# Seven-product steps, PSUM banks and token sums in a two-layer hybrid attention trunk

## The chip, the cores and the metric

The kernel runs on one core of one Trainium2 chip, as one launch. The metric is the device time of that core in microseconds (us), lower is better. A core has TensorE (PE), VectorE (DVE), ScalarE (ACT), GpSimd (POOL) and SyncE (SP), which issues most of the transfers, each with its own queue of instructions. PE writes its results into eight PSUM banks of 128 x 512 float32.

## The reference, cut to what matters

Two layers over 256 tokens of width 2048. In each layer one combined input projection feeds two groups of eight heads; their outputs are joined by an output projection; a SwiGLU block with inner width 5632 follows.

```python
for l in range(DEPTH):                       # 2
    h = rms_norm(x, pre_mix_norm[l])
    proj = h @ w_in[l]                       # 2048 -> 6144: q_sb, k_sb, v_sb, q_d, k_d, v_d
    o_sb = rms_norm(stick_breaking(q_sb, k_sb, v_sb), sb_out_norm[l])
    o_d = rms_norm(differential(rope(q_d), rope(k_d), v_d), diff_subln[l]) * (1 - lam_init)
    x = x + rms_norm(concat(o_sb, o_d) @ w_o[l], post_mix_norm[l])
    h = rms_norm(x, pre_ffn_norm[l])
    x = x + rms_norm((silu(h @ w_gate[l]) * (h @ w_up[l])) @ w_down[l], post_ffn_norm[l])
```

Stick-breaking attention needs, per pair of heads, scores, a log of the kept share, a product with a triangle of ones and an exponential. Differential attention needs two softmax maps per head, their difference, and a transpose of it before the product with v.

## The kernel before

**Products.** All projections are done in float32 by three products each. A weight block of 128 x 1024 (one K pair, that is two K tiles, of a chunk of 512 output columns) is loaded by one transfer of 512 KB into one of four `raw` buffers. ACT rounds it to `hi` (L247), DVE makes `lo` = raw - hi (L249), and `product` (L900) multiplies hi by hi, lo by hi and hi by lo (L903 to L905).

**Eight or seven.** Two chunks are worked together as a pair: for one K pair there are 2 token tiles x 2 chunks x 2 K tiles = 8 block products, 24 instructions (`eight_in`, L757). A Strassen-like form does it in seven, 21 instructions (`seven_in`, `seven_products`, L884 and L920). The seven need sums of weights (`mixed_weights`, L212: five operations of 512 columns and two of 1024 on DVE besides the lo of the first block, L225 to L232, L249, and the roundings on ACT, L221), sums of tokens made once per layer and K pair (`pair_forms` and `token_sums`, L767 and L907; in gate and up `pair_sums`, L1003), and four more banks `extra` for parts that several outputs share. `shared_part` (L937) brings these out once per pair (L940 to L944), and `settle` adds them to the accumulators (L794).

**Input projection.** `mixer_in` (L774) goes through six chunk pairs (`PAIRS`), each with eight K pairs. `IN_NOW[l][n]` lists the K pairs done as seven: none, three, two, two, two, none in layer 0; in layer 1 the first pair has two as well. Within pairs after the first, `IN_ORDER` puts 4, 5, 6 third to fifth. `opening` (L684) does the first pair of layer 0 and makes the token sums of that layer.

**Attention in between.** Attention runs as generators beside the projection. `tick` (L418) is called four times per K pair (every six or so products) and moves on each generator whose time has come: `flip` (L810) transposes q or k of a chunk, `stick_weights` (L536) and `diff_weights` (L594) make the weights of a head pair or a head, `attend` (L514) multiplies them by v, `norm_pair` (L478) normalizes and transposes the result into `mix`. A number that is yielded is a pause in ticks (2 without one). `run_until` in the output projection calls `tick` until the heads of the next K pair are in `mix`.

**PSUM.** Four banks are accumulators (`acc`), three are for passing use (`b`), one (`o`) is for attention's outputs. The sevens of the input projection take all three `b` and the `o`. `clear(n)` (L411) tells a generator whether n ticks are left before the next sevens start (`burst`). `claims[0]` lets one set of weights hold its two score banks at a time, `claims[1]` one attention output. Flips and other transposes take a bank without asking whether one is free.

**Gate and up.** Eleven chunk pairs; the first one works in the order `FIRST_ORDER` with kp 4 and 6 as seven, the first two K pairs being done ahead. `FORM_AT` says at which place among the remaining six (3, 2, 7, 4, 6, 5) the token sums of which K pair are issued.

**Order.** The program's text gives each instruction a place, but on each engine instructions whose inputs are expected to be ready are drawn forward past waiting ones; a stretch of the output projection has ACT and DVE kept in written order (L977), and `high_priority` moves the ends of chunks forward. `weights` (L257) feeds four blocks ahead.

Of the kernel before, what the change touches and what calls it, by code (L numbers as in the profile page):

```python
# [32 lines left out]
TAIL = 3  # L33
KP_O = (4, 5, 6, 7, 0, 1, 2, 3)
PAIRS = ((6, 8), (10, 7), (9, 0), (11, 2), (1, 3), (4, 5))
IN_SEVEN = (4, 5, 6)
IN_ORDER = (0, 1, 4, 5, 6, 2, 3, 7)
IN_NOW = tuple((first, (4, 5, 6), (4, 5), (4, 5), (4, 5), ()) for first in ((), (5, 6)))
SEVEN = (2, 4, 5, 6)
FIRST_SEVEN = (4, 6)  # L40
FIRST_ORDER = (0, 1, 3, 2, 7, 4, 6, 5)
FORM_AT = {1: 4, 2: 6, 4: 5, 5: 2}
DOWN_SEVEN = (3, 6, 9, 12, 15, 18)

WARM = 13
# [9 lines left out]
def weight_order():  # L55

    order = []

    def queue_pair(name, l, kp, c):
        order.append((name, l, kp, c))  # L60
        return len(order) - 1

    plan = []
    sevens, plain = set(), set()
    for l in range(L):
        lay = {"in": {}, "o": {}, "gate": {}, "up": {}, "down": {}}
        for n, (ca, cb) in enumerate(PAIRS):
            for kp in IN_ORDER if n else range(KT // 2):
                lay["in"][ca, kp] = queue_pair("w_in", l, kp, ca)
                lay["in"][cb, kp] = queue_pair("w_in", l, kp, cb)  # L70
                if kp in IN_NOW[l][n]:
                    plain.add(lay["in"][cb, kp])
        order_o = [(c, kp) for kp in KP_O for c in (0, 1)]
        order_o += [(c, kp) for c in (2, 3) for kp in range(KT // 2)]
        lay["order_o"] = order_o
        for c, kp in order_o:
            lay["o"][c, kp] = queue_pair("w_o", l, kp, c)
        for c in range(FF // CW):
            for kp in FIRST_ORDER if c == 0 else range(KT // 2):
                lay["gate"][c, kp] = queue_pair("w_gate", l, kp, c)  # L80
                lay["up"][c, kp] = queue_pair("w_up", l, kp, c)
                if kp in (FIRST_SEVEN if c == 0 else SEVEN):
                    sevens.add(lay["up"][c, kp])
        for half in range(2):
            for kp in range(FF // P // 2):
                for c in (2 * half, 2 * half + 1):
                    lay["down"][c, kp] = queue_pair("w_down", l, kp, c)
                if kp in DOWN_SEVEN:
                    sevens.add(lay["down"][2 * half + 1, kp])
        plan.append(lay)  # L90
    return order, plan, sevens, plain
# [48 lines left out]
def kernel(  # L140
# [264 lines left out]

    clock = [0]
    running = []
    burst = [None]
    claims = [0, 0]

    def clear(n):  # L411

        return burst[0] is None or clock[0] + n <= burst[0]

    def start(gen, n=1):
        running.append([clock[0] + n, gen])
# [61 lines left out]
    def norm_pair(pool, ob, mix, mixed, h0, gcol, nm):  # L478
        ss = small.tile([P, 4], F32, tag="oss", name=f"oss_{nm}")
        for i in range(4):  # L480
            junk = pool.tile([P, CW], F32, tag="t2", name=f"jo_{nm}_{i}")
            nc.scalar.activation(junk[:, 0:P], ob[:, i * P : (i + 1) * P], AF.Square, accum_out=ss[:, i : i + 1])
        yield
        rs = small.tile([P, 4], F32, tag="ors", name=f"ors_{nm}")
        rsqrt(rs, ss, 1.0 / P, nm)
        on = pool.tile([P, 4, P], F32, tag="t2", name=f"on_{nm}")
        nc.vector.tensor_tensor(
            out=on, in0=ob.rearrange("p (i d) -> p i d", i=4), in1=rs.unsqueeze(2).to_broadcast([P, 4, P]), op=ALU.mult
        )
        claims[1] -= 1  # L490
        yield
        yield
        while not clear(2):
            yield 1
        for j in range(2):
            mix[h0 + j] = pool.tile([P, 2, S], F32R, tag="mix" + nm[0], bufs=NH, name=f"mix_{nm}_{j}")
        pb = bank(f"oT_ps_{nm}")
        for i in range(4):
            nc.tensor.transpose(pb[:, i * P : (i + 1) * P], on[:, i, :], ident)
        for j in range(2):  # L500
            nc.scalar.activation(
                mix[h0 + j][:, 0, :], pb[:, j * S : (j + 1) * S], AF.Copy, scale=gains[:, gcol + j : gcol + j + 1]
            )
            nc.vector.scalar_tensor_tensor(
                out=mix[h0 + j][:, 1, :],
                in0=pb[:, j * S : (j + 1) * S],
                scalar=gains[:, gcol + j : gcol + j + 1],
                in1=mix[h0 + j][:, 0, :].bitcast(F32),
                op0=ALU.mult,
                op1=ALU.subtract,  # L510
            )
            mixed.add(h0 + j)

    def attend(pool, kind, l, g, st, mix, mixed):  # L514

        for hp in range(2):
            while (hp, 1) not in st["w"] or "v" not in st or claims[1] or not clear(4):
                yield 1
            claims[1] += 1
            nm = f"{kind}{l}_{g}_{hp}"  # L520
            ob = ps.tile([P, CW], F32, tag="o", bufs=1, name=f"o_{nm}")
            v = st["v"]
            for j in range(2):
                cols = slice((2 * hp + j) * P, (2 * hp + j + 1) * P)
                w = st["w"][hp, j]
                o0 = ob[:, j * S : j * S + P]
                o1 = ob[:, j * S + P : (j + 1) * S]
                nc.tensor.matmul(o0, w[0], v[:, 0, cols], start=True, stop=True)
                nc.tensor.matmul(o1, w[1], v[:, 0, cols], start=True, stop=False)
                nc.tensor.matmul(o1, w[2], v[:, 1, cols], start=False, stop=True)  # L530
            yield
            h0 = g * 4 + 2 * hp
            g0 = (64 if kind == "sb" else 80) + l * NH + h0
            yield from norm_pair(pool, ob, mix, mixed, h0 + (0 if kind == "sb" else NH), g0, nm)

    def stick_weights(pool, l, g, st):  # L536
        q, k = st["q"], st["k"]
        for hp in range(2):
            nm = f"sb{l}_{g}_{hp}"
            while claims[0] or not clear(10):  # L540
                yield 1
            claims[0] += 1
            za, zb = bank(f"za_{nm}"), bank(f"zb_{nm}")
            za3 = za.rearrange("p (h q) -> p h q", h=2)
            zb3 = zb[:, 0:S].rearrange("p (h q) -> p h q", h=2)
# [36 lines left out]
            nc.scalar.activation(w[:, 0 : 2 * S], za, AF.Exp)  # L582
            nc.scalar.activation(w[:, 2 * S : 2 * S + S], zb[:, 0:S], AF.Exp)
            yield
            claims[0] -= 1
            yield
            for j in range(2):
                st["w"][hp, j] = (
# [5 lines left out]
    def diff_weights(pool, l, g, st, j):  # L594

        q, k = st["q"], st["k"]
        for hp in range(2):
            h = 2 * hp + j
            nm = f"df{l}_{g}_{h}"
            while claims[0] or not clear(4):  # L600
                yield 1
            claims[0] += 1
            sc = [bank(f"s{m}_{nm}") for m in range(2)]
            for qt in range(2):
                for m in range(2):
# [31 lines left out]
                        accum_out=sm[:, c : c + 1],  # L637
                    )
            yield
            claims[0] -= 1  # L640
            nc.vector.reciprocal(sm, sm)
            nc.vector.tensor_tensor(out=sm, in0=sm, in1=lamsign[:, l, :], op=ALU.mult)
            for qt in range(2):
# [9 lines left out]
                )  # L653
            yield
            yield
            while not clear(2):
                yield 1
            tp = bank(f"pT_{nm}")
            for b in range(3):
# [114 lines left out]
    def mixer_in(pool, l, rs, xT, mix, mixed):  # L774
# [6 lines left out]

        for n, cc in enumerate(PAIRS):
            banks = [acc_bank(f"in{l}_{c}_{t}") for t in range(NT) for c in cc]
            mine = IN_NOW[l][n]
            w, toks = None, {}

            def settle(t):
# [22 lines left out]
            def flip(c, toks):  # L810
# [5 lines left out]
                key = "q" if kind in (0, 3) else "k"  # L816
                tT = st[key] = pool.tile([P, 4, S], F32, tag="qk", bufs=4, name=f"{key}T{l}_{c}")
                for t in range(NT):
                    while not clear(2):
                        yield 1  # L820
                    pb = bank(f"qkT_ps{l}_{c}_{t}")
                    for j in range(4):
                        nc.tensor.transpose(pb[:, j * P : (j + 1) * P], toks[c, t][:, j * P : (j + 1) * P], ident)
                    nc.scalar.copy(tT[:, :, t * P : (t + 1) * P], pb.rearrange("p (h q) -> p h q", h=4))
                    yield 1
                st[key + "done"] = True
                if "qdone" in st and "kdone" in st:
                    if kind < 3:
# [9 lines left out]
            else:  # L838
# [3 lines left out]
                for j, kp in enumerate(kps):  # L842
# [2 lines left out]
                        sums_of(IN_SEVEN[j - 2])  # L845
                    if kp in mine:
                        if extra is None:
                            assert claims[0] == 0
                            extra = four_banks(True, [f"{q}_in{l}_{n}" for q in ("p1", "p6", "p7", "q5")])
                        seven_in(banks, extra, forms[kp], xT, l, cc, kp, kp == mine[0], kp == mine[-1])  # L850
                        if kp == mine[-1]:
                            burst[0] = None
                            w = pool.tile([P, 4, CW], F32, tag="gpost", bufs=1, name=f"w{l}_{n}")
                            shared_part(extra, [w[:, i, :] for i in range(4)])
                            if n + 1 < len(PAIRS) and IN_NOW[l][n + 1]:
                                burst[0] = clock[0] + 4 * (len(kps) - 1 - j) + 4 * IN_ORDER.index(IN_NOW[l][n + 1][0])
                            else:
                                pool.end_of_sums()
                        continue
# [18 lines left out]
            wait = 3  # L878
            for c in cc:
                if c // 2 not in (2, 5):  # L880
                    start(flip(c, toks), wait if c // 2 < 3 else wait + 6)
                    wait += 2

    def seven_in(banks, extra, sums, xT, l, cc, kp, first, last):  # L884
        hi, lo = weights(plan[l]["in"][cc[0], kp], LOOKAHEAD)
# [339 lines left out]
```

## Time and profile before

| what | value |
|---|---|
| device time, median of 3 runs | 2235.07 us (2230.51 to 2238.75) |
| device time of the profiled execution | 2233.99 us |
| its span, first to last instruction | 2232.3 us |
| granted TensorE clock, mean | 0.996 |
| input projection of layer 0 / layer 1 | 6.8 to 309.4 us / 1110.4 to 1422.5 us |
| gate and up start, layer 0 / layer 1 | 404.3 us / 1517.4 us |
| HBM read, written | 456.47 MB, 8.39 MB |

A row of a group of instructions names the line, engine and operation, the tile written and the tiles read, shape, count, busy time and mean duration in ns, and the idle time of the engine before them with what ended it. A row of waits reads "engine and instruction <- what it waited for: us in total, times, longest". A row of windows gives the busy time and the count of instructions of each engine in that stretch. The chain of waits ends with PE at 77% of the span, DVE at 13% and transfers at 4%. Idle time of an engine that does not set the end costs nothing.

### The profile page before, as it was taken

To read this page: it belongs to the slowest core of one execution; us is meant where nothing else is said; L and a number is where in the kernel's file an instruction comes from. 1 tells how busy PE (TensorE), PEld (TensorE's weight loads), DVE (VectorE), ACT (ScalarE), POOL (GpSimd) and SP (SyncE) were. 2 spreads that over 40 slices of the span, in tenths; PEclk is the share of its full clock that TensorE was granted. 3 is DMA by queue.
4 is the path that set the end of the run, shared out by engine and by line. 5 is a ranking of instruction groups with operands and counts; after the bars stand their busy time and mean duration, and the time that the engine had idled before them with its cause. 6 is when DMAs were issued, how large, how long until landed. Compare 5 with 4: busy or idle time off the path is not lost.

```text
span 2232.3 us, 28660 instructions
## 1 busy us (share of the span) xinstructions
PE 2192.2 (98%) x9997; PEld 1790.3 (80%) x9997; DVE 1896.3 (85%) x2718; ACT 1363.4 (61%) x2041; POOL 137.6 (6%) x184
## 2 busy tenths in 40 slices
PE   9999999999999999999989999999999999999998
PEld 7777888778888888888867778887788888888886
DVE  7888655899999998989899886558999999989897
ACT  7666654656655656656666666546566566566663
POOL 1100000000000000000002000000000000000000
PEclk9999999999999999999999999999999999999999
DMA  8555655787776675767455556557867767757673
GB/s 288 171 170 164 214 189 183 227 256 220 224 248 212 221 245 188 243 205 240 156 183 162 172 173 200 184 191 237 248 212 233 234 213 232 234 193 246 198 254 100
DMA packets 138081, 466.75 MB, mean 209 GB/s; under 512 B 15824, under 2 KB 16336, under 8 KB 137424
## 3 DMA queue, kind: packets, MB, share of 16 engines
q1 hardware_dynamic: 120512, 430.30, 56.4%
q0 software_dynamic: 15552, 28.32, 7.7%
q10 hardware_dynamic: 1872, 6.31, 0.7%
q8 instruction: 78, 1.28, 0.2%
q14 instruction: 67, 0.55, 0.1%
HBM read 456.47 MB, written 8.39 MB: 208 GB/s over the span
## 4 chain that ended last, share of the span: by engine, by line
PE 77%; DVE 13%; DMA 4%; issue 3%; ACT 2%; SPq 0%; DVEq 0%; ACTq 0%
PE c L904 8%; PE c L905 8%; PE c L903 8%; PE in L903 5%; PE in L905 5%; PE in L904 5%; PE dn L1109 4%; PE dn L1110 4%; PE dn L1112 4%; DMA raw<-in_weights_in_turn_dram 4%; DVE lo L249 4%; PE o L441 3%; PE o L443 3%; PE o L442 3%; PE p L903 2%
## 5 line engine op out<-in xcount | busy, mean ns | idle before, releaser
L249 DVE TENSOR_TENSOR lo<-raw,hi 128x1024 fp32r<-128x1024 f32 x546 | 657.7, 1223 | 164.8 <-ACT hi L247 163.9
L247 ACT ACTIVATE hi<-raw 128x1024 fp32r<-128x1024 f32 x546 | 565.5, 1053 | 254.0 <-DMA raw<-in_weights_in_turn_dram 75.5
L903 PE MATMUL c<-hi,xF 128*128 128x512 f32 x820 | 323.0, 396 | 4.3 <-DVE w L944 2.2
L904 PE MATMUL c<-lo,xF 128*128 128x512 f32 x820 | 320.4, 392 | 3.7 <-DVE lo L249 3.7
L905 PE MATMUL c<-hi,xF 128*128 128x512 f32 x820 | 319.7, 392 | 0.0
L207 POOL DMA_DIRECT2D T<-in_weights_in_turn_dram x108 | 94.1, 871 | 1671.4 <-DMA T<-in_weights_in_turn_dram 560.4
L903 PEld LDWEIGHTS c<-hi,xF 128*128 128x128 f32 x820 | 154.1, 188 | 37.7 <-ACT hi L247 3.3
L904 PEld LDWEIGHTS c<-lo,xF 128*128 128x128 f32 x820 | 155.0, 189 | 35.2 <-DVE lo L249 4.6
L905 PEld LDWEIGHTS c<-hi,xF 128*128 128x128 f32 x820 | 154.9, 189 | 32.7
L1109 PE MATMUL dn<-hi,jh 128*128 128x512 f32 x464 | 180.7, 389 | 0.0
L1110 PE MATMUL dn<-lo,jh 128*128 128x512 f32 x464 | 180.5, 389 | 0.0
L249 DVE TENSOR_TENSOR lo<-G,hi 128x1024 fp32r<-128x1024 f32 x108 | 131.7, 1220 | 27.8 <-ACT hi L247 27.7
L221 ACT ACTIVATE Th<-T 128x512 fp32r<-128x512 f32 x108 | 67.6, 626 | 128.0 <-DVE T L228 128.0
L1112 PE MATMUL dn<-hi,jl 128*128 128x512 f32 x464 | 142.9, 389 | 0.0
L222 DVE TENSOR_TENSOR lo<-T,hi 128x1024 fp32r<-128x1024 f32 x108 | 131.7, 1220 | 12.1 <-ACT hi L221 11.5
L222 DVE TENSOR_TENSOR Tl<-G,Th 128x1024 fp32r<-128x1024 f32 x108 | 131.7, 1220 | 9.3 <-ACT Th L221 9.2
L221 ACT ACTIVATE hi<-T 128x1024 fp32r<-128x1024 f32 x108 | 113.3, 1049 | 42.3 <-PE c L905 25.1
L221 ACT ACTIVATE Th<-G 128x1024 fp32r<-128x1024 f32 x108 | 113.9, 1054 | 39.1 <-DVE G L230 38.9
L903 PE MATMUL in<-hi,xT 128*128 128x512 f32 x321 | 128.2, 401 | 0.3 <-ACT xT L695 0.3
L903 PE MATMUL in<-hi,xI 128*128 128x512 f32 x307 | 123.3, 405 | 4.4 <-DVE w L794 3.4
L904 PE MATMUL in<-lo,xT 128*128 128x512 f32 x321 | 125.9, 392 | 0.7 <-DVE lo L249 0.7
L905 PE MATMUL in<-hi,xT 128*128 128x512 f32 x321 | 125.7, 392 | 0.0
(376 smaller groups left out, 4705.6 us busy)
## 6 DMA issues: line engine op xcount, KB each, us to landing
raw<-in_weights_in_turn_dram SPq DMA_DIRECT2D x566, 512.0 KB, 4.5
T<-in_weights_in_turn_dram SPq DMA_DIRECT2D x108, 512.0 KB, 4.5
G<-in_weights_in_turn_dram SPq DMA_DIRECT2D x108, 512.0 KB, 4.7
T<-in_weights_in_turn_dram POOLq DMA_DIRECT2D x108, 256.0 KB, 6.4
away_ffn<-x ACTq DMA_DIRECT2D x8, 512.0 KB, 5.4
xd<-away_ffn SPq DMA_DIRECT2D x8, 512.0 KB, 9.3
xr<-in_x_columns_dram SPq DMA_DIRECT2D x8, 256.0 KB, 6.4
x<-in_x_dram SPq DMA_DIRECT2D x8, 256.0 KB, 6.5
```

The source lines that it names most:

```text
L207: nc.gpsimd.dma_start(sums[i][:, 0, :], stream[i - 1][:, 0, :], accum_op=ALU.add)
L221: nc.scalar.activation(h, w, AF.Copy)
L222: nc.vector.tensor_tensor(out=l, in0=w, in1=h.bitcast(F32), op=ALU.subtract)
L247: nc.scalar.activation(hi, raw, AF.Copy)
L249: nc.vector.tensor_tensor(out=lo, in0=raw, in1=hi.bitcast(F32), op=ALU.subtract)
L441: nc.tensor.matmul(a, sh, hi[:, kk, :], start=first and kk == 0, stop=False)
L903: nc.tensor.matmul(a, sh, hi, start=first, stop=False)
L904: nc.tensor.matmul(a, sh, lo, start=False, stop=False)
L905: nc.tensor.matmul(a, sl, hi, start=False, stop=last)
L1109: nc.tensor.matmul(accs[c, t], sh, hi[:, kk, :], start=first, stop=False)
L1110: nc.tensor.matmul(accs[c, t], sh, lo[:, kk, :], start=False, stop=False)
L1112: nc.tensor.matmul(accs[c, t], sl, hi[:, kk, :], start=False, stop=last)
```

## The change

K pair 6 is no longer done as seven in the second chunk pair of both layers, and K pairs 5 and 6 no longer in the first chunk pair of layer 1, so that `IN_NOW` is the same in both layers: two K pairs in each of the four middle chunk pairs. Token sums of the input projection are made for K pairs 4 and 5 alone.

`claims` goes. `taken` lists until which tick each `b` bank is counted as held, and `banks_for(n, ticks, held)` lets a generator go on only if n more fit into three and `clear(ticks)` holds. A bank for a transpose counts for two ticks; the two of a set of weights count until `give_back`, and one tick more. Flips ask for each of their two banks and pause two ticks after each, and start later: the second of a pair three ticks after the first instead of two, and for the differential heads 4 x (number of sevens in the next pair) ticks later. After the last seven of a pair, `clear` is false for `SETTLE` = 2 ticks.

In the first chunk pair of gate and up the token sums of K pairs 4 and 6 are issued one place later; those of 5 and 2 stay.

```diff
 TAIL = 3
 KP_O = (4, 5, 6, 7, 0, 1, 2, 3)
 PAIRS = ((6, 8), (10, 7), (9, 0), (11, 2), (1, 3), (4, 5))
-IN_SEVEN = (4, 5, 6)
+IN_SEVEN = (4, 5)
 IN_ORDER = (0, 1, 4, 5, 6, 2, 3, 7)
-IN_NOW = tuple((first, (4, 5, 6), (4, 5), (4, 5), (4, 5), ()) for first in ((), (5, 6)))
+IN_NOW = ((), IN_SEVEN, IN_SEVEN, IN_SEVEN, IN_SEVEN, ())
+SETTLE = 2
 SEVEN = (2, 4, 5, 6)
 FIRST_SEVEN = (4, 6)
 FIRST_ORDER = (0, 1, 3, 2, 7, 4, 6, 5)
-FORM_AT = {1: 4, 2: 6, 4: 5, 5: 2}
+FORM_AT = {2: 4, 3: 6, 4: 5, 5: 2}
 DOWN_SEVEN = (3, 6, 9, 12, 15, 18)
 
 WARM = 13
...
             for kp in IN_ORDER if n else range(KT // 2):
                 lay["in"][ca, kp] = queue_pair("w_in", l, kp, ca)
                 lay["in"][cb, kp] = queue_pair("w_in", l, kp, cb)
-                if kp in IN_NOW[l][n]:
+                if kp in IN_NOW[n]:
                     plain.add(lay["in"][cb, kp])
         order_o = [(c, kp) for kp in KP_O for c in (0, 1)]
         order_o += [(c, kp) for c in (2, 3) for kp in range(KT // 2)]
...
 
     clock = [0]
     running = []
-    burst = [None]
-    claims = [0, 0]
+    burst = [None, 0]
+    attending = [0]
 
     def clear(n):
 
-        return burst[0] is None or clock[0] + n <= burst[0]
+        return clock[0] >= burst[1] and (burst[0] is None or clock[0] + n <= burst[0])
+
+    taken = []
+
+    def banks_for(n, ticks, held=False):
+
+        taken[:] = [until for until in taken if until > clock[0]]
+        if len(taken) + n > 3 or not clear(ticks):
+            return False
+        taken.extend([math.inf if held else clock[0] + 2] * n)
+        return True
+
+    def give_back():
+        taken[:] = [clock[0] + 1 if until == math.inf else until for until in taken]
 
     def start(gen, n=1):
         running.append([clock[0] + n, gen])
...
         nc.vector.tensor_tensor(
             out=on, in0=ob.rearrange("p (i d) -> p i d", i=4), in1=rs.unsqueeze(2).to_broadcast([P, 4, P]), op=ALU.mult
         )
-        claims[1] -= 1
+        attending[0] -= 1
         yield
         yield
-        while not clear(2):
+        while not banks_for(1, 2):
             yield 1
         for j in range(2):
             mix[h0 + j] = pool.tile([P, 2, S], F32R, tag="mix" + nm[0], bufs=NH, name=f"mix_{nm}_{j}")
...
     def attend(pool, kind, l, g, st, mix, mixed):
 
         for hp in range(2):
-            while (hp, 1) not in st["w"] or "v" not in st or claims[1] or not clear(4):
+            while (hp, 1) not in st["w"] or "v" not in st or attending[0] or not clear(4):
                 yield 1
-            claims[1] += 1
+            attending[0] += 1
             nm = f"{kind}{l}_{g}_{hp}"
             ob = ps.tile([P, CW], F32, tag="o", bufs=1, name=f"o_{nm}")
             v = st["v"]
...
         q, k = st["q"], st["k"]
         for hp in range(2):
             nm = f"sb{l}_{g}_{hp}"
-            while claims[0] or not clear(10):
+            while math.inf in taken or not banks_for(2, 10, True):
                 yield 1
-            claims[0] += 1
             za, zb = bank(f"za_{nm}"), bank(f"zb_{nm}")
             za3 = za.rearrange("p (h q) -> p h q", h=2)
             zb3 = zb[:, 0:S].rearrange("p (h q) -> p h q", h=2)
...
             nc.scalar.activation(w[:, 0 : 2 * S], za, AF.Exp)
             nc.scalar.activation(w[:, 2 * S : 2 * S + S], zb[:, 0:S], AF.Exp)
             yield
-            claims[0] -= 1
+            give_back()
             yield
             for j in range(2):
                 st["w"][hp, j] = (
...
         for hp in range(2):
             h = 2 * hp + j
             nm = f"df{l}_{g}_{h}"
-            while claims[0] or not clear(4):
+            while math.inf in taken or not banks_for(2, 4, True):
                 yield 1
-            claims[0] += 1
             sc = [bank(f"s{m}_{nm}") for m in range(2)]
             for qt in range(2):
                 for m in range(2):
...
                         accum_out=sm[:, c : c + 1],
                     )
             yield
-            claims[0] -= 1
+            give_back()
             nc.vector.reciprocal(sm, sm)
             nc.vector.tensor_tensor(out=sm, in0=sm, in1=lamsign[:, l, :], op=ALU.mult)
             for qt in range(2):
...
                 )
             yield
             yield
-            while not clear(2):
+            while not banks_for(1, 2):
                 yield 1
             tp = bank(f"pT_{nm}")
             for b in range(3):
...
 
         for n, cc in enumerate(PAIRS):
             banks = [acc_bank(f"in{l}_{c}_{t}") for t in range(NT) for c in cc]
-            mine = IN_NOW[l][n]
+            mine = IN_NOW[n]
             w, toks = None, {}
 
             def settle(t):
...
                 key = "q" if kind in (0, 3) else "k"
                 tT = st[key] = pool.tile([P, 4, S], F32, tag="qk", bufs=4, name=f"{key}T{l}_{c}")
                 for t in range(NT):
-                    while not clear(2):
+                    while not banks_for(1, 2):
                         yield 1
                     pb = bank(f"qkT_ps{l}_{c}_{t}")
                     for j in range(4):
                         nc.tensor.transpose(pb[:, j * P : (j + 1) * P], toks[c, t][:, j * P : (j + 1) * P], ident)
                     nc.scalar.copy(tT[:, :, t * P : (t + 1) * P], pb.rearrange("p (h q) -> p h q", h=4))
-                    yield 1
+                    yield 2
                 st[key + "done"] = True
                 if "qdone" in st and "kdone" in st:
                     if kind < 3:
...
                         sums_of(IN_SEVEN[j - 2])
                     if kp in mine:
                         if extra is None:
-                            assert claims[0] == 0
+                            assert math.inf not in taken
                             extra = four_banks(True, [f"{q}_in{l}_{n}" for q in ("p1", "p6", "p7", "q5")])
                         seven_in(banks, extra, forms[kp], xT, l, cc, kp, kp == mine[0], kp == mine[-1])
                         if kp == mine[-1]:
-                            burst[0] = None
+                            burst[:] = None, clock[0] + SETTLE
                             w = pool.tile([P, 4, CW], F32, tag="gpost", bufs=1, name=f"w{l}_{n}")
                             shared_part(extra, [w[:, i, :] for i in range(4)])
-                            if n + 1 < len(PAIRS) and IN_NOW[l][n + 1]:
-                                burst[0] = clock[0] + 4 * (len(kps) - 1 - j) + 4 * IN_ORDER.index(IN_NOW[l][n + 1][0])
+                            if n + 1 < len(PAIRS) and IN_NOW[n + 1]:
+                                burst[0] = clock[0] + 4 * (len(kps) - 1 - j) + 4 * IN_ORDER.index(IN_NOW[n + 1][0])
                             else:
                                 pool.end_of_sums()
                         continue
...
             wait = 3
             for c in cc:
                 if c // 2 not in (2, 5):
-                    start(flip(c, toks), wait if c // 2 < 3 else wait + 6)
-                    wait += 2
+                    start(flip(c, toks), wait if c // 2 < 3 else wait + 6 + 4 * len(IN_NOW[n + 1]))
+                    wait += 3
 
     def seven_in(banks, extra, sums, xT, l, cc, kp, first, last):
         hi, lo = weights(plan[l]["in"][cc[0], kp], LOOKAHEAD)
```

## The prediction

> **What bounds the kernel now.** First the page: how busy each engine is.
>
> ```profile
> PE 2192.2 (98%) x9997; PEld 1790.3 (80%) x9997; DVE 1896.3 (85%) x2718; ACT 1363.4 (61%) x2041; POOL 137.6 (6%) x184
> ```
>
> TensorE (PE) is drawn as always busy, but a product is drawn 0.39 us long while the next one starts earlier, so its pace must be read from counts. Hence the windows of 20 us (length; then busy time and count of PE, its weight loads, VectorE (DVE), ScalarE (ACT), GpSimd; granted clock; DMA share; GB/s), and windows laid over chunk pairs, whose borders come from the time line: pairs 0 and 1 of layer 0, then of layer 1.
>
> ```profile
> 360.00:380.00 20.00, 20.00 (x90) 16.57 (x89) 9.86 (x10) 8.34 (x8) 0.00 (x0) 1.00 0.62 197
> 420.00:440.00 20.00, 17.36 (x67) 13.19 (x66) 18.63 (x46) 12.56 (x24) 1.90 (x3) 0.91 0.97 328
> 1140.00:1160.00 20.00, 17.04 (x71) 12.30 (x70) 18.31 (x29) 11.05 (x13) 0.00 (x0) 1.00 0.41 130
> 1160.00:1180.00 20.00, 16.59 (x66) 13.24 (x65) 18.05 (x22) 10.60 (x13) 12.25 (x16) 0.91 0.44 146
> ...
> 6.80:51.90 45.10, 44.35 (x192) 35.98 (x193) 37.70 (x90) 33.42 (x61) 2.74 (x7) 1.00 0.95 315
> 51.90:102.40 50.50, 48.78 (x227) 37.00 (x225) 44.06 (x63) 32.43 (x51) 10.32 (x16) 1.00 0.58 186
> 1110.40:1165.20 54.80, 47.81 (x215) 36.88 (x215) 50.18 (x115) 35.66 (x78) 0.00 (x0) 1.00 0.56 187
> 1165.20:1215.70 50.50, 49.84 (x226) 37.94 (x226) 45.94 (x67) 32.46 (x52) 14.42 (x20) 0.97 0.55 177
> ```
>
> Undisturbed, PE takes 90 products in 20 us: **0.222 us each**. Where the count falls below 90, DVE is at 18 of 20: there DVE sets the end. Pair 0 of layer 1 takes 54.8 us; its 186 products at 0.222 (41.3) and 28 transposes, of which four take 0.36 (2.5), come to 43.8. So that pair alone loses 11 us. Who ends the waits of PE (us, times, longest):
>
> ```profile
> PE c L904 <- DVE lo L249: 3.7, 2, 1.8
> PE in L903 <- DVE w L794: 3.4, 1, 3.4
> PE p_in L903 <- ACT Th L221: 2.7, 2, 1.6
> PE qkT_ps L823 <- ACT qT L824: 2.5, 2, 1.3
> PE oT_ps_df L499 <- DVE w L941: 2.3, 2, 1.2
> PE q_in L903 <- ACT hi L221: 1.1, 1, 1.1
> ```
>
> And the time line of PE around the longest of them (start, duration, line, [idle before]):
>
> ```profile
> 1161.36 0.39 PE L905 MATMUL in<-hi,xI 128*128 128x512 f32 x1
> 1165.16 0.47 PE L903 MATMUL in<-hi,xI 128*128 128x512 f32 x1 [3.41 <-DVE w L794]
> ...
> 1167.22 0.63 PE L904 MATMUL in<-lo,xI 128*128 128x512 f32 x1
> 1167.64 0.63 PE L905 MATMUL in<-hi,xI 128*128 128x512 f32 x1
> ```
>
> After that wait products start 0.43 apart for 3.4 us (1166.4 to 1169.8): half clock, 1.7 us lost. A wait costs its idle time plus 0.17 (0.39 drawn less 0.22 pace).
>
> **The change, part by part.** Sums are made against the profiled execution: 2232.3 span, 2234.0 with what lies around it; the median shown is 2235.1, 1.1 higher.
>
> (A) *Four seven-product steps become eights* (kp 6 in pair 1 of both layers, kp 5 and 6 in pair 0 of layer 1): 24 products for 21, so 4 x 3 x 0.222 = **+2.7 us** on PE. No transfer is added or removed: the weights of both forms are the same 512 KB loads on the same queue.
>
> (B) *What DVE is spared.* An eight has two subtractions of 1024 columns, one every 1.14 us (four L249 in a row take 4.62): 2.3. A seven has three of these (lo, lo, Tl) and five of 512 columns, one every 0.60 (L225, L228, L229, L230, Tl): 6.4, against 21 x 0.222 = 4.7 of PE. So DVE falls 1.7 behind in each seven and gains 3.0 in each eight. The change takes 4 x 4.1 = 16.5 from DVE, one set of token sums per layer (two L771 0.34, four of 128 columns 0.20, one L917 0.60: 2.1), and in pair 0 of layer 1 the four adds of shared_part and the four of L794 (8 x 0.60 = 4.8). DVE does not bound the whole, so only the waits count. In pair 0 of layer 1 those after 1140 are 1.6 (p_in), 1.1 (q_in), 0.2 (hi), 0.2 (Tl) and 3.4 (w L794, the accumulator that pair 1 needs): 6.5 + 5 x 0.17 = 7.4. Without a seven in that pair none of these operations exists, its accumulators go out through ScalarE alone, and DVE has 43 us for 16 subtractions and two sets of sums (22 us) besides the layer change: **-7.4**, bounds -5 to -8.4 (the 11 lost less 2.6 in the first 26 us, which belong to the layer change). The half-clock spell of 1166 goes with its cause: **-1.7**.
>
> (C) *Pair 1 with two sevens for three.* Its waits are 1.1 (Th) and 0.6 (kT) in layer 0, 0.5 (hi) and some tenths in layer 1: some 3.3 with the 0.17 each. The two sevens that stay still come first, at the same tick: I take **-2.0**, bounds 0 to -3.3.
>
> (D) *Banks counted, flips later.* In the old code the tick after the sevens (81 and 145 of layer time) asks for up to five banks of three: a transpose of weights, two score banks, two flips. PE then stands in order behind ScalarE's copy of qT (1.3 and 1.2), or behind L941 emptying the banks of the sevens (1.0 and 1.2), or kT (0.3 and 0.4): 5.4 + 6 x 0.17 = 6.4. Counting ticks through the yields, the new code spreads the same requests over ticks 82 to 91 and 146 to 159, and SETTLE holds all for 2 ticks (2.7 us). But the four adds L941 to L944 took from 83.8 to 89.1, 5.3 us, between other DVE work, so SETTLE covers half: **-4.0**, bounds +2.5 (as many waits elsewhere, a single score block held by a late bank in each layer) to -6.4. Waiting costs nothing as long as products cover it: the last triangle of stick-breaking moves from tick 188 to 194, its product with v stays at 206, and the output projection's loop adds no empty tick before or after.
>
> (E) *Sums for gate and up one unit later.* The waits at the start of gate and up, 0.6, 0.2 and 1.85 for hi and lo (2.65 + 0.5), with a half-clock spell (1.7), are 4.9 per layer. What DVE does then:
>
> ```profile
> 422.49 0.42 DVE L1007 TENSOR_TENSOR f<-xF 128x256 f32<-128x256 f32 x1
> ...
> 425.38 0.42 DVE L1007 TENSOR_TENSOR f<-xF 128x256 f32<-128x256 f32 x1
> ...
> 426.45 4.62 DVE L249 TENSOR_TENSOR lo<-raw,hi 128x1024 fp32r<-128x1024 f32 x4
> ```
>
> Sums run for 4 us while PE waits for lo. But three sets started there, the third (425.38) from a unit that the program has two units later than these lo: the order on an engine is not the program's, a ready operation is drawn forward. Moved by one unit, the first two remain nearer than the third was. I take **0**. Bounds: -9.8 (all of it goes in both layers) to +9.0 (sums late for the first seven: f, s, sh, sl, 2.8 us, and a half-clock spell, per layer).
>
> Sum: 2.7 - 7.4 - 1.7 - 2.0 - 4.0 + 0 = -12.4; the smaller relief on DVE in pairs 2 (it enters without a debt) rounds it to **-13**: span 2219.3, 2221 with its margin, **2222** beside the median.
>
> On the clock: spells follow 3.4 us idle in one piece, and 2.6 in three pieces within 4.3; 1.6 and 1.1 at 1147 to 1152 were followed by none. So length alone does not decide, and everything after the first 100 us moves by several us: each of the spells at 429 and 1542 can go, or one more can come, 1.7 each way; this is in the range. The Trainium skill ("TensorE: Matmul & The Clock Gate", Part 1) says that the gate halves the clock after an idle window of about 3.4 us and that the window runs freely. By that rule the spells at 429 and 1542 would not be there at all; the trace has them (0.91 granted at 420 to 440), so the rows decide, while a spell of 3.4 us at half clock agrees.
>
> **Rivals.** *1. Gate and up gain too.* If the later place puts lo first on DVE, E gives up to 9.8, say 8.6: 2222 - 8.6 = 2213. For it: DVE has no slack there; against: the drawn-forward third set. *2. The wait moves.* DVE is 18 of 20 busy for the whole layer change, and if it enters pair 1 with its debt, pair 1 takes over the waits for Th, hi and w L794: B and the spell give nothing, 2222 + 9 = 2231. Against: 3.0 us gained on every one of eight eights. *3. Slower: attention is pushed past its cover.* Holding two banks at a time from a count of three, and flips that start at tick 17 instead of 9 after their pair, delay the weights of the last heads by 6 ticks (8 us). The margin before their product with v is 12 ticks, 16 us, was 18. Each bank that frees late pushes the rest; from more than 12 ticks on, PE has only the output projection's next step, which needs those heads. Six ticks over in each layer and a spell: 2 x (8 + 1.7) = 19.4, less 13: 2241. Against: DVE is at 24.65 of 52.7 us in pair 5, ScalarE at 31.15. *4. Nothing reaches the end*, every gain eaten by the added products: 2235.
>
> **Chances.** Forecast 0.48 (2217 to 2228), rival 1 0.17, rival 2 0.16, rival 3 0.10, rival 4 0.09. Within 0.5% (11 us, what a measurement of this kernel can tell from no change) means 2223.9 to 2246.2. Faster: rival 1 and three quarters of the forecast, 0.53; slower by over 0.5%: most of rival 3 grown further, 0.09; the rest 0.38. Range 2211 to 2238; the forecast's own is above.
>
> **What would show it.** 12 more products; pair 0 of layer 1 at 48 to 49 us with no wait for w L794 and full clock at 1160; no wait of qkT_ps or oT_ps of over 0.5; DVE busy some 25 us less; lo before f at the start of gate and up only if rival 1 holds; in the output projection no wait for mix. Pair 0 of layer 1 above 52 us, or a wait for mix, would make it wrong.

## The result, and the profile after

| | before | changed kernel |
|---|---|---|
| device time, median of 5 runs each | 2234.2 us (2230.51 to 2238.75) | 2224.13 us (2221.83 to 2225.03) |
| ratio, 95% interval | | 0.9955 [0.9938, 0.9972] |
| span of the profiled execution | 2232.3 us | 2223.3 us |

The change makes the kernel some 10 us faster, 3 less than forecast. In one profile a stage is known only to some 2 us: in a second profile of the changed kernel (e12 below) pairs 1 to 5 take 254.3 and 252.2 us and pair 0 of layer 0 takes 45.1, while pair 0 of layer 1 takes 48.1 again. Where the time went is read from the starts of the first product of each part in the time lines of PE (us):

| part | before | changed | difference |
|---|---|---|---|
| layer 0: pair 0 | 45.1 | 44.3 | -0.9 |
| layer 0: pairs 1 to 5 | 257.5 | 255.2 | -2.3 |
| layer 0: output projection | 94.8 | 95.8 | +1.0 |
| layer 0: gate and up; down | 471.6; 234.5 | 472.2; 236.8 | +0.6; +2.2 |
| layer 1: pair 0 | 54.7 | 48.1 | -6.6 |
| layer 1: pairs 1 to 5 | 257.4 | 254.9 | -2.5 |
| layer 1: output projection | 94.8 | 95.8 | +1.0 |
| layer 1: gate and up; down | 471.7; 243.2 | 470.8; 243.0 | -0.9; -0.3 |

The start itself is 0.2 shorter. First the page of the changed kernel, then its windows over pairs 0 and 1 of layer 0 and of layer 1.

```profile
PE 2189.9 (98%) x10009; PEld 1796.3 (81%) x10009; DVE 1869.2 (84%) x2672; ACT 1353.8 (61%) x2030; POOL 133.8 (6%) x184
```

```profile
6.59:50.80 44.21, 44.21 (x192) 36.00 (x193) 35.70 (x83) 33.02 (x60) 2.54 (x6) 1.00 0.88 315
50.80:99.30 48.50, 47.15 (x222) 37.41 (x222) 40.07 (x57) 28.07 (x43) 9.73 (x15) 1.00 0.64 211
1110.80:1158.90 48.10, 47.49 (x221) 38.71 (x222) 40.45 (x95) 33.31 (x75) 2.28 (x5) 1.00 0.68 229
1158.90:1205.50 46.60, 46.60 (x221) 37.56 (x220) 37.15 (x53) 26.86 (x42) 9.77 (x14) 1.00 0.57 186
```

PE has 12 products more and DVE 27 us less. Pair 0 of layer 1 is 6.6 us shorter with six more instructions in its window, DVE's busy time in it falls from 50.2 to 40.5, and pair 1 runs at full clock: the wait for w L794 and its half-clock spell are gone, and nothing took their place there. The waits of PE in the changed kernel (its lines stand 12 further on here, 1 for lo, hi, Th and Tl):

```profile
PE s_df L619 <- DVE w L954: 4.2, 4, 1.5
PE c L916 <- DVE lo L250: 3.7, 2, 1.8
PE c L915 <- DVE w L956: 3.1, 2, 1.6
...
PE o_df L542 <- DVE w L956: 1.3, 2, 1.1
PE p_in L915 <- ACT Th L222: 1.2, 1, 1.2
...
PE qkT_ps L835 <- DVE w L953: 0.8, 1, 0.8
```

q_in and the longest p_in are gone, as forecast. The waits for qT and L941 are gone too, but score products (s_df), attention's outputs (o_df) and flips now wait 6.3 us (3.6 in the second profile) for L953, L954 and L956: the adds of `shared_part` that empty the banks of the sevens. With the new bank rules waits on banks have not gone, they have other names. The next time lines are of the changed kernel, DVE, ACT and then PE, at the end of the sevens of pair 2 in layer 0; the first PE row is the last product of these sevens.

```profile
121.95 0.68 DVE L953 TENSOR_TENSOR w<-p_in,w 128x512 f32<-128x512 f32 x1
123.47 1.23 DVE L250 TENSOR_TENSOR lo<-raw,hi 128x1024 fp32r<-128x1024 f32 x1 [0.83 <-ACT hi L248]
124.61 0.68 DVE L954 TENSOR_TENSOR w<-p_in,w 128x512 f32<-128x512 f32 x1
125.59 1.22 DVE L250 TENSOR_TENSOR lo<-raw,hi 128x1024 fp32r<-128x1024 f32 x1 [0.30 <-ACT hi L248]
126.73 0.68 DVE L955 TENSOR_TENSOR w<-q_in,w 128x512 f32<-128x512 f32 x1
127.33 0.68 DVE L956 TENSOR_TENSOR w<-q_in,w 128x512 f32<-128x512 f32 x1
```

```profile
122.37 1.06 ACT L248 ACTIVATE hi<-raw 128x1024 fp32r<-128x1024 f32 x1 [1.60 <-DMA raw<-in_weights_in_turn_dram]
```

```profile
121.30 0.39 PE L917 MATMUL in<-Th,xT 128*128 128x512 f32 x1
...
123.31 0.49 PE L619 MATMUL s_df<-kT,qT 64*128 64x128 f32 x2
125.34 0.92 PE L619 MATMUL s_df<-kT,qT 64*128 64x128 f32 x6 [1.54 <-DVE w L954]
...
128.06 0.49 PE L542 MATMUL o_df<-v,pT 128*128 128x128 f32 x2 [0.21 <-DVE w L956]
```

Four adds that would take 2.4 us back to back take from 121.95 to 128.0, because two lo stand between them in DVE's order and wait 0.83 and 0.30 for their hi; the first of these hi had itself waited for its weights to land (1.60). The sevens end at 121.7. The second score bank comes free with L954 at 125.3, 3.6 us later, and PE, which works in order, stands until then; the bank for attention's outputs comes free with L956 at 128.0, 6.3 us later. In the changed kernel's time lines of all eight pairs with sevens L954 ends 3.0 to 4.9 us after the last product of the sevens (0.8 in pair 1 of layer 0), and L956 5.1 to 7.2. SETTLE of 2 ticks is 2.7 us. The Trainium skill ("TensorE: Matmul & The Clock Gate", Part 1) calls VectorE's queue strictly first in, first out; these rows agree, since DVE idles before a lo with a ready add behind it.

### The profile page after: what moved, and what is told of

It reads as the page before. It is cut to its first block, busy times and chain, and to the rows that moved or that the text cites. A ratio compares the mean times of both kernels' runs of the same rounds, so it can differ in the third digit from the quotient of the medians.

```text
span 2223.3 us, 28639 instructions
## 1 busy us (share of the span) xinstructions
PE 2189.9 (98%) x10009; PEld 1796.3 (81%) x10009; DVE 1869.2 (84%) x2672; ACT 1353.8 (61%) x2030; POOL 133.8 (6%) x184
## 4 chain that ended last, share of the span: by engine, by line
PE 80%; DVE 10%; DMA 4%; issue 3%; ACT 2%; DVEq 0%; ACTq 0%; SPq 0%
PE c L916 8%; PE c L917 8%; PE c L915 8%; PE in L915 5%; PE in L916 5%; PE in L917 5%; PE dn L1122 5%; PE dn L1121 5%; PE dn L1124 5%; DMA raw<-in_weights_in_turn_dram 4%; DVE lo L250 3%; PE o L457 3%; PE o L455 3%; PE o L456 3%; PE p L915 2%
## 5 line engine op out<-in xcount | busy, mean ns | idle before, releaser
L915 PE MATMUL in<-hi,xT 128*128 128x512 f32 x328 | 131.3, 401 | 0.3 <-ACT xT L707 0.3
L915 PE MATMUL in<-hi,xI 128*128 128x512 f32 x328 | 131.3, 402 | 0.2 <-ACT xI L374 0.2
L916 PE MATMUL in<-lo,xI 128*128 128x512 f32 x328 | 128.3, 392 | 0.3 <-DVE lo L250 0.3
L917 PE MATMUL in<-hi,xT 128*128 128x512 f32 x328 | 128.5, 392 | 0.0
```

The lines of the kernel that those rows point to most:

```text
L915: nc.tensor.matmul(a, sh, hi, start=first, stop=False)
L916: nc.tensor.matmul(a, sh, lo, start=False, stop=False)
L917: nc.tensor.matmul(a, sl, hi, start=False, stop=last)
```

## The experiments

Each ratio is against runs of the kernel before on the same chip. Three chips were used (e1 to e4, e5 to e8, e9 to e12), so runs from different groups are compared by their ratios.

**The parts alone.** The kernel before with the new sevens only (e1):

```diff
-IN_SEVEN = (4, 5, 6)
+IN_SEVEN = (4, 5)
-IN_NOW = tuple((first, (4, 5, 6), (4, 5), (4, 5), (4, 5), ()) for first in ((), (5, 6)))
+IN_NOW = (((), (4, 5), (4, 5), (4, 5), (4, 5), ()),) * 2
```

> The kernel before with the new choice of sevens alone (two K pairs in the four middle chunk pairs, token sums for 4 and 5); bank rules and the place of gate and up's sums as before. Theory 1 (relief of VectorE is the whole gain): -8.4 us by the forecast's terms A, B and C, a little more by the stages of the two traces (first pair of layer 1 -6.6, second pairs -3.9 and -2.0): -8 to -12, at or below the changed kernel's time. Rival (the bank rules carry part of it): -4 or less. Rival 2 of the prediction (the waits move on into the second pair): -2 to 0.

Measured: 2220.18, ratio 0.9949 [0.9936, 0.9963], -10.4 us. The sevens alone give as much as the whole change. Pair 0 of layer 1 takes 48.1 us. The waits on the emptying adds in later pairs are there with the old bank rules too (qkT 3.4, oT 1.9 us), and longer than the 2.3 of the kernel before.

The kernel before without the sevens of the first pair of layer 1 (e2):

```diff
-IN_NOW = tuple((first, (4, 5, 6), (4, 5), (4, 5), (4, 5), ()) for first in ((), (5, 6)))
+IN_NOW = tuple((first, (4, 5, 6), (4, 5), (4, 5), (4, 5), ()) for first in ((), ()))
```

> Only the two sevens of the first chunk pair of layer 1 become eights; three sevens stay in the second pairs. If that pair alone carries the relief: 1.3 - 7.4 - 1.7 = -7.8 us, pair 0 of layer 1 at 48 to 49 us, no half clock at 1160. If the wait moves: pair 0 short, but pair 1 of layer 1 longer by as much, and 0 to -3 in total.

Measured: 2225.1, ratio 0.9973 [0.9962, 0.9983], -5.5 us: about half of the gain of e1 comes from two steps of one pair. That is 2.3 less than expected, though the interval (-3.8 to -8.5 us) has room for the -7.8. The pair takes 48.1 for 54.7, no spell at 1160. In part the wait did move on: pair 1 of layer 1 is 51.1 us for 50.6, though the spell no longer falls into it, with new waits for Th and Tl (0.7 and 1.4). Pair 2 is 52.2 for 50.7 because a half-clock spell now falls there (at 1231). So rival 2 holds for a part, as long as pair 1 keeps its third seven.

The changed kernel with the sevens and the place of the sums of the kernel before (e3):

```diff
-IN_SEVEN = (4, 5)
+IN_SEVEN = (4, 5, 6)
-IN_NOW = ((), IN_SEVEN, IN_SEVEN, IN_SEVEN, IN_SEVEN, ())
+IN_NOW = tuple((first, (4, 5, 6), (4, 5), (4, 5), (4, 5), ()) for first in ((), (5, 6)))
-FORM_AT = {2: 4, 3: 6, 4: 5, 5: 2}
+FORM_AT = {1: 4, 2: 6, 4: 5, 5: 2}
```

> The bank rules alone (count of three banks, two ticks of rest after the sevens, later flips), with the old choice of sevens and the old place of gate and up's sums. The forecast's term D: -4 us. What the two traces suggest instead (the waits on L954 and L956 of the changed kernel sum to as much as the waits on qT and L941 of the one before, and each output projection is 1 us longer): +1 to +3.

Measured: 2230.34, ratio 1.0 [0.999, 1.0009]. The bank rules as they stand are worth nothing that these runs can tell from zero (within 2 us); the forecast's -4 falls, and of the loss that the two traces suggested only its upper part is excluded.

The kernel before with the place of the sums alone (e4):

```diff
-FORM_AT = {1: 4, 2: 6, 4: 5, 5: 2}
+FORM_AT = {2: 4, 3: 6, 4: 5, 5: 2}
```

> Only the token sums of gate and up one place later. The forecast's term E: 0, since a ready operation is drawn forward; the order of instructions on every engine is then the same as before, so this run is also a measure of how far two equal programs differ: within 2 us. Rival 1: -5 to -10.

Measured: 2230.0, ratio 1.0 [0.999, 1.0011]. The order of the instructions on PE, DVE, ACT, GpSimd and SyncE is the same, line for line, as in the kernel before, so this edit alone cannot bring the gain of rival 1.

**How long to rest after the sevens.** The changed kernel with 4 (e5), 0 (e6) and 6 ticks (e11). The first edit is shown; in the others the number is 0 or 6.

```diff
-SETTLE = 2
+SETTLE = 4
```

> The changed kernel with SETTLE = 4 ticks (5.3 us) instead of 2, which is as long as the four adds that empty the banks of the sevens took (83.8 to 89.1). Theory (the waits of s_df, o_df and qkT on L953 to L956, 6.3 us of idle time, are attention asking for banks before these adds are done): those waits fall to under 2 us and the time by 3 to 6 us. Rival (a delayed attention meets other banks late): the waits change names, time within 2 us.

> The changed kernel with SETTLE = 0. Theory: attention asks for the banks at once after the sevens, the waits on L953 to L956 grow by 2.7 us at each of four places per layer where they bind, some 5 to 10 us in all. Rival (the planner of each engine's order, not this rule, decides when attention's products come): within 2 us.

> The changed kernel with SETTLE = 6. The adds are done after 4 ticks, so there is nothing more to gain there, while attention's last weights come later still: 0 to +4 beside the run with SETTLE = 4. If banks still free late at 4 ticks: -1 to -3.

Measured: with 4 ticks 2214.48, ratio 0.992 [0.9907, 0.9934]; with 0, 2227.52, 0.9982 [0.9973, 0.9991]; with 6, 2216.13, 0.9921 [0.9908, 0.9934]. By the ratios each tick from 0 to 4 is worth some 3 to 4 us, and then there is nothing more. That fits the time lines above: 2.7 us of rest is shorter than the 3.0 to 4.9 after which the third passing bank is free in seven of the eight pairs, and 5.3 us is longer. At 4 ticks the waits on the emptying adds fall from 6.3 to 0.7 us (o_df L542 on L956) and pairs 1 to 5 take 251.2 and 249.7 us for 255.2 and 254.9 (254.3 and 252.2 in the second profile). The gain, 7 us, is a little above the 3 to 6 expected. At 0 ticks the score products wait 1.2 for L953 and 4.5 for a copy by ACT out of another passing bank: not the releaser that was expected, but the same three banks.

**Which bank rule it is (e9).** The new sevens with the bank rules of the kernel before (`claims`, early flips) and nothing but the rest of 4 ticks, on the kernel with the sevens alone.

```diff
+SETTLE = 4
-        return burst[0] is None or clock[0] + n <= burst[0]
+        return clock[0] >= burst[1] and (burst[0] is None or clock[0] + n <= burst[0])
...
-                            burst[0] = None
+                            burst[:] = None, clock[0] + SETTLE
```

> The new sevens, the bank rules of the kernel before, and only a rest of 4 ticks after the sevens. If the rest is what the run with SETTLE = 4 gained, this is as fast: 2213 to 2217 beside 2231. If the count of banks and the later flips are needed with it: 2218 or more, with waits of qkT and za on banks.

Measured: 2214.54, ratio 0.9915 [0.9903, 0.9928], span 2210.9. It is as fast as the run with all rules. The waits of PE in this run:

```profile
PE c L905 <- DVE lo L250: 3.7, 2, 1.9
PE c L904 <- DVE w L945: 2.4, 2, 1.2
PE c L904 <- ACT hi L248: 1.6, 4, 0.6
...
PE p_in L904 <- ACT Th L222: 0.6, 1, 0.6
```

No wait on an emptying add of the input projection is left; the rows shown are of gate and up (tile c), and the last is the wait for Th in the input projection. So the count of three banks, the give-back and the later flips are not needed for this gain: the rest is. Without a rest these rules even cost something: the changed kernel with SETTLE = 0 has 0.9982 [0.9973, 0.9991], the sevens alone with the old rules 0.9949 [0.9936, 0.9963], some 7 us less. With two ticks of rest the new rules are as fast as the old ones with none, and with four ticks the two sets are equal. Which of the new rules costs this was not tried.

The changed kernel once more (e12):

> The changed kernel once more, on the same chip as the three above: 2220 to 2224 beside 2231, 6 to 9 us slower than the run with SETTLE = 4.

Measured: 2221.47, ratio 0.9949 [0.9936, 0.9961], 7 us slower than e9 and 5 us slower than the run with 6 ticks, all on this chip.

**The old sevens with the long rest (e10)**, on the kernel with the bank rules alone.

```diff
-SETTLE = 2
+SETTLE = 4
```

> The old sevens (20 of them) with the new bank rules and a rest of 4 ticks. If the two parts add: the sevens cost 10 more than in the run with SETTLE = 4, so 2224 to 2227. If a longer rest also hides what VectorE is behind: under 2220. If it lets the third seven's debt meet the shorter remainder of the pair: 2228 or more.

Measured: 2227.52, ratio 0.9974 [0.9963, 0.9984]. By the ratios the old sevens cost 12 us beside the same rules with the new ones (0.9974 and 0.992), where e1 had 10: within the noise the parts add. In its waits w L806 (the accumulators of pair 1, 3.1 us), q_in (1.0) and two of p_in (2.7) are back.

**Gate and up's sums behind lo.** The token sums are tied behind the last lo issued ahead of them, in the changed kernel (e7) and in the one with the sevens alone (e8).

```diff
-            nc.vector.tensor_tensor(out=lo, in0=raw, in1=hi.bitcast(F32), op=ALU.subtract)
+            last_lo[0] = nc.vector.tensor_tensor(out=lo, in0=raw, in1=hi.bitcast(F32), op=ALU.subtract)
...
-                    pair_sums(FORM_AT[n])
+                    with tc.issue_after(last_lo[0].ins):
+                        pair_sums(FORM_AT[n])
```

> The changed kernel with the token sums of gate and up tied behind the last subtraction (lo) that was issued ahead of them, so that VectorE can no longer draw them forward. Theory (the sums at 420 to 424 delay lo, and PE's wait of 1.85 with the half-clock spell is their price): lo runs about 2 us earlier, that wait and the spell go, -2 to -6 us over both layers. Rival: the sums are missed later, a new wait of the first sevens of gate and up for sl or Tl takes their place, 0 to +5.

> The kernel before with the new choice of sevens alone and the same tie for gate and up's sums: without the new bank rules. If the bank rules are worth nothing or cost a little, this is as fast as the run before it or 1 to 3 us faster, and the fastest of all so far (2214 to 2218 beside 2231 for the kernel before); if they help, it is 2 to 4 us slower than that run.

Measured: e7 2227.25, ratio 0.9982 [0.9973, 0.9991], against 0.9955 and 0.9949 of the changed kernel; e8 2223.87, 0.9962 [0.9948, 0.9975], against 0.9949 of the sevens alone, so its forecast was missed by 6 us. The waits of PE from 400 to 480 us in e7:

```profile
PE c L916 <- ACT Th L223: 1.7, 2, 1.3
PE c L917 <- DVE Tl L224: 0.9, 1, 0.9
PE c L916 <- ACT hi L249: 0.8, 2, 0.6
```

The wait for lo is gone, but waits for Th and Tl of the first sevens of gate and up stand in its place, and gate and up takes 475.5 and 473.2 us for 472.2 and 470.8 (472.4 and 472.2 in the second profile of the changed kernel). By these rows the sums that DVE does while PE waits are work that it lacks time for later. e8 cannot be told from the sevens alone, as the intervals overlap.

## Why the prediction was right, and where not

The forecast was 2222 us and -13; it came to 2224 and -10. That it came so near is in part luck: the -4.0 of D did not come, while the sevens, A to C, gave -10.4 by e1 where the forecast had -8.4. By its steps:

- **A, the added products**: right. The count of PE rises by 12.
- **B, pair 0 of layer 1**: right in mechanism and size. Forecast 48 to 49 us with full clock; measured 48.1. With its 1.3 of added products that is -8.0 against -7.4, and the spell of 1.7 is gone besides. The pair takes 48.1 in each of the ten profiles of kernels without its sevens. In e2, where those sevens alone go, 5.5 of the expected 7.8 is left in the whole, as part of the waits moves into pair 1.
- **C, two sevens in pair 1**: right in direction, and too small by the runs. The sevens alone shorten pairs 1 to 5 of layer 0 by 1.9 us with the 0.7 of added products in it, 2.6 without; in layer 1 these pairs stay as long as before, because a wait of 2.0 for L941 with a spell at 1174.6 comes in where the spell of 1166 was. e1 and e2 differ by the third sevens of pair 1 and their token sums alone, and by 4.9 us (known to some 4), where the forecast had 1.3 - 2.0 = -0.7. The waits that the forecast named come to 3.3 in all. Part of the remainder is that the waits for Th and Tl, which e2 moves into pair 1 of layer 1, are gone in e1; where the rest comes from stays open.
- **D, banks counted**: wrong in size, though inside its bounds (+2.5 to -6.4). "-4.0" was taken for the spread of requests and SETTLE; the bank rules alone measure 0 (ratio 1.0), and the changed kernel is not faster than the sevens alone. The old waits went as foreseen (qT, L941), and the prediction had itself read that the four adds take 5.3 us and that SETTLE covers 2.7. It named as many waits elsewhere as a bound and took most of the old ones as gained; they came. The third passing bank, which the second block of scores needs, is free only 3.0 to 4.9 us after the sevens in most pairs. Resting for 4 ticks gives a further 7 us.
- **E, sums one unit later**: right, 0. The third set drawn forward was the clue; the order on every engine does not change at all, and the wait of 1.8 stands at both starts of gate and up as before. The clock spells, expected to come and go by 1.7 each, are one fewer in gate and up (1542) and one more in the down projection (896); in the second profile of the same kernel both of these are the other way round, so this is chance.

Rival 1 falls with e4, where the order stays, and with e7, where lo does come first and the kernel is slower. Rival 4 falls with the result. Rival 3 did not come: no wait for mix is in the trace, and each output projection is only 1 us longer, where the last triangle now stands (454 instructions of PE for 448). Rival 2 is seen in part in e2 alone.

The fastest runs of this study are the new sevens with a rest of 4 ticks: 2214.5 us with either set of bank rules, 0.992 and 0.9915 of the kernel before, faster than both kernels. What was not tried: emptying the banks faster by putting the four adds ahead of the lo that stand between them.

## What to carry to other kernels

An algorithm that saves products pays only where the engine that makes its sums has time: count both engines for each stage, and leave the cheaper form out of the stages where the other engine is behind (here two steps of one pair were worth about half of the gain). When a burst takes all passing banks, hold the next users back until the banks are really empty, by the measured length of the emptying in that order of instructions and not by the sum of its operations. And where the order on an engine is chosen by readiness, moving a step by one place in the program may change nothing: compare the orders before giving it a price.

## What the runs showed of the hardware

Half-clock spells do not follow from the length of a wait alone. In two profiles of the changed kernel, with the same order of instructions, all four starts of gate and up have the same waits of PE (1.8 or 1.9 for lo and 0.8 for hi). What follows differs; windows of the first profile, then one of the second (e12), with the granted clock third from the end:

```profile
420.00:440.00 20.00, 17.36 (x68) 13.30 (x67) 18.74 (x41) 13.18 (x17) 1.74 (x2) 0.91 0.90 291
1520.00:1540.00 20.00, 17.36 (x79) 13.41 (x78) 17.85 (x55) 12.57 (x32) 1.75 (x2) 1.00 0.95 319
```

```profile
1520.00:1540.00 20.00, 17.37 (x63) 13.12 (x62) 18.94 (x45) 11.47 (x17) 1.75 (x2) 0.83 0.97 317
```

The busy time of PE is the same to a hundredth or two, with 68, 79 and 63 instructions: one spell, none, and one of double length. The run e4, whose order is that of the kernel before, has a spell at 501 after a wait of 2.3 where the kernel before had 1.5 and none. The Trainium skill ("TensorE: Matmul & The Clock Gate", Part 1) says that the window of the gate runs freely; that agrees. Its rule there that the clock falls after an idle window of about 3.4 us does not agree: here 2.6 us of idle time in three pieces is enough in most places, and spells also follow single waits of 2.0 (e1, at 1174.6), 1.7 (the changed kernel, at 896) and 1.1 us (e2, at 1231, among short attention products and transposes).

Apart from the last 10 us of the span, a spell lasts 3.4 us in the records of the granted clock, or 6.8 (e12 from 1525.6), so it costs up to 1.7 or 3.4. Executions of equal orders differ by such sums: the down projection of layer 0 takes 236.8 us in the first profile of the changed kernel, with a spell and a wait of 1.7 for Tl before it, and 233.0 in the second, with neither.
